# A hybrid encoder block: triangular inverses of two head groups at a time on 128 lanes, and an output projection over all tokens with its inputs finished by heads

## The chip, the core and the metric

The kernel runs on one core of a Trainium2 chip. A core has a matrix engine (TensorE, PE in the profile, with its weight loads listed as PEld), three engines for elementwise work (VectorE or DVE, ScalarE or ACT, GpSimd or POOL), and SyncE (SP), which here only issues transfers. Each engine runs its own instructions in order; semaphores tie them together. Transfers are issued from the queues of SP, POOL and ACT and are carried out by 16 DMA engines. The metric is the device time of one execution in microseconds (us); lower is better.

## The reference

One layer of a block with 512 tokens (S) and 1024 channels (D). After a normalisation, a wide projection `p = h @ w_in` feeds three mixers; their outputs are gated, added and projected, and a squared-ReLU MLP follows:

```python
y_a = b_a * causal_dwconv(c_a * x_a, conv_a_w)
y_b = rg_lru(causal_dwconv(x_b, ...), ...) * gelu(g_b)
yc  = rwkv7_recurrence(r, decay, k, v, kk, a)      # 16 heads of 64
y_c = (layernorm_per_head(yc) * lnx_g + lnx_b + bonus) * g_c
m   = gate_a * y_a + gate_b * y_b + gate_c * y_c
x   = x + m @ w_out
x   = x + square(relu(rms_norm(x) @ mlp_w1)) @ mlp_w2
out = rms_norm(x)
```

The recurrence over tokens is computed in 8 chunks (NC) of 64 tokens (L). Within a chunk it needs, per head, the inverse of a unit triangular 64x64 matrix: 8 chunks times 16 heads are 128 such matrices.

## The kernel before, in words

*Precision.* Every large product is made from three matmuls (`mm3`, L166): the operands are split into a high and a low part, and hi\*hi, hi\*lo, lo\*hi are added. Weights come in tiles of 128x1024: `load_w` (L132) issues the transfer from SP, ScalarE casts the high part `whi` (L146) and VectorE subtracts to get the low part `wlo` (L147, through the helper at L103). There are two raw buffers and three of each part. A projection of 128 output channels (`proj`, L306) is 24 matmuls over 512 tokens into one of three accumulation buffers (`pp`).

*Stages.* The 16 heads are worked on in four groups (NG). For each group, `krv` (L418) projects k, r and v and prepares the scaled operands AR and BK. `amat` (L517) forms the chunk matrices into the tile AXt and writes them to DRAM (`axd`, `bkd`). `inverse(g)` (L546) inverts the group's 32 matrices. Then `chain` (L628) walks through the eight chunks with the state, `norm` (L694) normalises the results in Y after every second chunk, and `fin_m` (L708) turns Y to channels and merges it with the gates. In between, as filler, run `ab(q)` (L744), the first two mixers for each of eight channel tiles q (29 steps each, 232 in all), and `gate(q)` (L726), the projection of the third gate (four steps each). Their results are in the tiles BV and GQ, each in two halves of 256 tokens.

*An inverse.* The 32 matrices of a group lie on lanes: la has one matrix per lane and diagonal block (two blocks of 32x32 per matrix, 64 lanes). Two transposes from AXt fill la (L553). Then 31 substitution steps of two VectorE operations each, a product into dg and a sum into Z, work on all lanes at once (L559 to L568). Three transposes bring the inverses back (L575, L580). The off-diagonal 32x32 block is made on PE by 32 small products pG (L587) and 32 small products pT (L597), each with a copy on ScalarE, and the whole goes to DRAM (`ttd`, L600), from where `load_chunk` reads it per chunk.

*The order of the work.* The program's order is a list by priority, made by hand. `weave(crit, fill, r)` (L823) advances a critical generator by one `yield`, at a raised priority, and then the filler by r steps on average. The filler of an inverse is `fill_group` of the next group (30 steps of `ab`, then `krv` with 9 more among its steps, then 3), at 0.8 steps per step; the last inverse has `ab` steps at 0.85. `N_TT`, `NINV`, `NG_T` are empty steps of the inverse: so many yields lie between its transposes, between the last one and pG, and between pG and pT. `keep_in_program_order` and `pin` fix single instructions in their place. The chain runs with 1.6 filler steps per step over what is left of `ab` and then the gates.

*The output projection* (L900 to L933) is woven by token halves: when the first four chunks are normalised and the gates are done, `fin_m(0, 4)` finishes the first 256 tokens of all heads, and the first three output tiles (W3) are accumulated over them; `fin_m(4, 8)` and the second half follow, then the other five tiles, each as two halves of 256 columns.

Of the kernel before, what the change touches and what calls it, by code (L numbers as in the profile page):

```python
# [18 lines left out]
P = 128  # L19
# [5 lines left out]
N_TT, NINV, NG_T, N_LOAD = 2, 12, 4, 6  # L25


N_KRV = 22
F_INV, F_KRV, F_GAP = 30, 9, 3
W3 = 3  # L30
R0, R1, R2, R3, R4 = 0.85, 0.8, 0.85, 1.6, 1.0
# [66 lines left out]
def block_kernel(ctx, tc, xt, win, par, mulr, sw, wout, w1, w2, fg, cst, eyes, out):  # L98
# [118 lines left out]
    sp = gr_ctx.enter_context(tc.tile_pool(name="sp", bufs=1))  # L217

    HT = S // 2
    HALF = [slice(th * HT, (th + 1) * HT) for th in range(2)]  # L220

    def bv_tile(q, th, dt=F32):
        return sp.tile([P, HT], dt, tag=f"bv{q}{th}", name="bv" if dt == F32 else "ml", align_bytes=AL)
# [194 lines left out]
    def krv(g, G_):  # L418
# [98 lines left out]
    def amat(g, G_):  # L517

        G_.AX = p1.tile([P, 2, NC, 4, L], F32, tag="AXt", name="AXt")
        for c4 in range(2):  # L520
# [10 lines left out]
            yield  # L531
        gp.dma_start(axd[:, 0:64, g, 1].rearrange("c s e t -> s c (e t)"),
# [13 lines left out]
    def inverse(g, G_):  # L546
        AXt = G_.AX
        Z = p1.tile([P, 2, 32, 32], F32, tag="Z", name="Z")
        la, xt = Z[64:128, 0], Z[64:128, 1]
        dg = p1.tile([P, 32, 32], F32, tag="dg", name="dg")  # L550
        tmp = dg[64:128].rearrange("p a b -> p (a b)")
        for b in range(2):
            v.transpose(la[32 * b:32 * b + 32].rearrange("l s t -> l t s"),  # L553
                        AXt[32 * b:32 * b + 32, 0, :, :, 32 * b:32 * b + 32].rearrange("s c e t -> s t (c e)"))
# [576 lines left out]
```

## Time and profile before

| what | value |
|---|---|
| median of three runs | 1103.43 us (1099.84 to 1107.11) |
| the profiled execution's own time | 1100.19 us |
| its span, first to last instruction | 1098.4 us |
| mean granted clock of TensorE | 0.979 |
| moved by DMA | 142.13 MB, mean 129 GB/s |

The profile is one execution. It lists for each engine the busy time and its share of the span, shows the span in 40 equal slices with the busy tenths of each engine, and names groups of instructions by line, engine and operation as `out<-in`, with count, busy time, the mean duration of one in ns, and the idle time before them with what ended it. PEclk is the clock that was granted to TensorE, 9 standing for 0.9 or more. Matmuls are pipelined, so their listed durations overlap; how many run in a stretch of time tells their pace. A line can be a helper's: L103, L106 and L109 are the VectorE helpers, L167 to L169 the three matmuls of `mm3`. A float32 matmul appears as two instructions.

### The profile page before, as it was taken

To read this page: it belongs to the slowest core of one execution; us is meant where nothing else is said; L and a number is where in the kernel's file an instruction comes from. 1 tells how busy PE (TensorE), PEld (TensorE's weight loads), DVE (VectorE), ACT (ScalarE), POOL (GpSimd) and SP (SyncE) were. 2 spreads that over 40 slices of the span, in tenths; PEclk is the share of its full clock that TensorE was granted. 3 is DMA by queue.
4 is the path that set the end of the run, shared out by engine and by line. 5 is a ranking of instruction groups with operands and counts; after the bars stand their busy time and mean duration, and the time that the engine had idled before them with its cause. 6 is when DMAs were issued, how large, how long until landed. Compare 5 with 4: busy or idle time off the path is not lost.

```text
span 1098.4 us, 16103 instructions
## 1 busy us (share of the span) xinstructions
PE 1053.0 (96%) x6396; PEld 863.2 (79%) x6396; DVE 735.3 (67%) x1266; ACT 486.4 (44%) x718; POOL 93.7 (9%) x159
## 2 busy tenths in 40 slices
PE   8999989999999979999699998999999999999996
PEld 5777867787877867788578886998888888888885
DVE  7998987899788987889547777855444443222224
ACT  7755455444573545363445444334444443111114
POOL 0011001110111002200031210101000000000001
PEclk9999989999999989999799999999999999999999
DMA  6336324452446224453288753334332335333232
GB/s 219 120 95 183 100 81 131 130 158 87 138 127 172 82 85 123 123 159 105 70 265 256 252 196 104 116 111 158 96 96 96 96 96 192 96 96 96 95 97 76
DMA packets 43323, 142.13 MB, mean 129 GB/s; under 512 B 5680, under 2 KB 9264, under 8 KB 42224
## 3 DMA queue, kind: packets, MB, share of 16 engines
q1 hardware_dynamic: 29472, 91.02, 25.9%
q0 software_dynamic: 13056, 49.03, 14.8%
q8 instruction: 50, 0.82, 0.3%
q10 hardware_dynamic: 720, 1.05, 0.3%
q14 instruction: 25, 0.20, 0.1%
HBM read 115.91 MB, written 25.17 MB: 128 GB/s over the span
## 4 chain that ended last, share of the span: by engine, by line
PE 47%; DVE 2%; ACT 1%; issue 1%; DMA 0%; DVEq 0%; ACTq 0%
PE acc L167 7%; PE acc L168 7%; PE acc L169 7%; PE p L168 5%; PE p L169 5%; PE p L167 5%; PE pp L167 2%; PE pp L169 2%; PE pp L168 2%; PE py L654 1%; PE pu L644 1%; PE pu L664 1%; PE pS L673 1%; PE pG L587 0%; DVE xr L106 0%
## 5 line engine op out<-in xcount | busy, mean ns | idle before, releaser
L103 DVE TENSOR_TENSOR wlo<-raw,whi 128x1024 fp32r<-128x1024 f32 (+1 forms) x164 | 197.9, 1208 | 228.5 <-ACT whi L146 222.7
L146 ACT CAST whi<-raw 128x1024 fp32r<-128x1024 f32 (+1 forms) x164 | 169.6, 1035 | 274.7 <-PE acc L169 125.0
L167 PE MATMUL pp<-hh,whi 128*128 128x512 f32 x688 | 275.1, 400 | 7.2 <-ACT g L799 4.2
L169 PE MATMUL pp<-hh,wlo 128*128 128x512 f32 x688 | 273.4, 397 | 2.7 <-DVE wlo L103 2.7
L168 PE MATMUL pp<-hl,whi 128*128 128x512 f32 x688 | 273.6, 398 | 0.0
L167 PEld LDWEIGHTS pp<-hh,whi 128*128 128x128 f32 x688 | 131.2, 191 | 37.0 <-ACT g L799 4.8
L169 PEld LDWEIGHTS pp<-hh,wlo 128*128 128x128 f32 x688 | 131.2, 191 | 32.3 <-DVE wlo L103 4.8
L168 PEld LDWEIGHTS pp<-hl,whi 128*128 128x128 f32 x688 | 131.3, 191 | 27.0
L167 PE MATMUL p<-h2h,whi 128*128 128x512 f32 (+1 forms) x264 | 101.4, 384 | 0.0
L168 PE MATMUL p<-h2l,whi 128*128 128x512 f32 (+1 forms) x264 | 101.2, 383 | 0.0
L169 PE MATMUL p<-h2h,wlo 128*128 128x512 f32 (+1 forms) x264 | 101.1, 383 | 0.0
L167 PE MATMUL acc<-whi,ah 128*128 128x512 f32 x256 | 99.6, 389 | 0.0
L168 PE MATMUL acc<-wlo,ah 128*128 128x512 f32 x256 | 99.6, 389 | 0.0
L169 PE MATMUL acc<-whi,al 128*128 128x512 f32 x256 | 99.6, 389 | 0.0
L167 PEld LDWEIGHTS p<-h2h,whi 128*128 128x128 f32 x264 | 49.6, 188 | 9.7
L168 PEld LDWEIGHTS p<-h2l,whi 128*128 128x128 f32 x264 | 49.7, 188 | 9.5
L169 PEld LDWEIGHTS p<-h2h,wlo 128*128 128x128 f32 x264 | 49.6, 188 | 9.6
L169 PEld LDWEIGHTS acc<-whi,al 128*128 128x128 f32 x256 | 48.0, 188 | 10.1
L167 PEld LDWEIGHTS acc<-whi,ah 128*128 128x128 f32 x256 | 48.0, 188 | 10.0
L168 PEld LDWEIGHTS acc<-wlo,ah 128*128 128x128 f32 x256 | 48.0, 188 | 9.9
L103 DVE TENSOR_TENSOR dg<-Z 64x31 f32<-64x31 f32 (+15 forms) x124 | 42.2, 340 | 4.1
L103 DVE TENSOR_TENSOR Z<-Z,dg 64x31 f32<-64x31 f32 (+15 forms) x124 | 42.2, 340 | 4.1
(304 smaller groups left out, 1465.7 us busy)
## 6 DMA issues: line engine op xcount, KB each, us to landing
raw<-in_win SPq DMA_DIRECT2D x88, 512.0 KB, 3.5
raw<-in_w SPq DMA_DIRECT2D x64, 512.0 KB, 3.5
ax<-axd POOLq DMA_DIRECT2D x8, 1024.0 KB, 7.5
axd<-AXt POOLq DMA_DIRECT2D x12, 512.0 KB, 7.1
bkd<-BKT POOLq DMA_DIRECT2D x4, 1024.0 KB, 12.4
raw<-in_wout SPq DMA_DIRECT2D x8, 512.0 KB, 3.6
bk<-bkd POOLq DMA_DIRECT2D x7, 512.0 KB, 8.5
swr<-in_sw SPq DMA_DIRECT2D x16, 128.0 KB, 2.3
```

What stands on the lines that cost most here:

```text
L103: return v.tensor_tensor(out=o, in0=a, in1=b, op=op)
L146: ac.copy(hi[:, sl], raw[:, sl])
L167: pe.matmul(ps, wh, xh, start=start, stop=False)
L168: pe.matmul(ps, wh, xl, start=False, stop=False)
L169: pe.matmul(ps, wl, xh, start=False, stop=stop)
L644: pin(n, lambda: pe.matmul(pu[64 * h:64 * h + 64, x], ax[rows, g, 0, e], sv[rows, g, e], start=True, stop=True))
L654: pin(behind, lambda: pe.matmul(py[64 * h:64 * h + 64, x], w, y, start=first and x == 0, stop=last, skip_group_check=True))
L664: pin(n, lambda: pe.matmul(pu[64 * h:64 * h + 64, x], tc_[:, g, e], u0[:, g, e], start=True, stop=True))
L673: pin(n, lambda: pe.matmul(pS[64 * h:64 * h + 64, x], bk[:, x, 64 * h:64 * h + 64], sv[:, g, e], start=True, stop=True))
```

## The change

Groups are inverted in pairs, on 128 lanes: `inverse(0)` for groups 0 and 1 is woven into the filler of group 2, and `inverse(1)` for groups 2 and 3 stands where the last inverse stood. The list la is no longer made by transposes from AXt. Instead `amat` writes the diagonal blocks of each group to DRAM (`lad`, two transfers of 32 lines by 32 runs of 128 B) and the off-diagonal ones (`odd`, one transfer), and `inverse` loads la from there, with 8 empty steps (`N_LA`) before the first substitution step. One transpose over 128 lanes takes the place of two over 32 for the way back, one over 64 lanes makes d1, and 24 empty steps instead of 12 lie ahead of pG. The small products alternate between the two groups, which lie on different row and column quarters of the array. `ttd` gets another layout; its diagonal blocks are written straight after the transpose, its off-diagonal ones after pT, and its zero blocks once, early.

BV and GQ become tiles of all 512 tokens. `fin_m(g)` finishes the two channel tiles of one group over all tokens. Once the chain's program has ended, it is called after a gate for each group whose gates are done, and for the others after the last gate. The output projection then runs in one piece, eight tiles of 24 matmuls over 512 tokens. The filler shares change with it (`FILL`).

```diff
-N_TT, NINV, NG_T, N_LOAD = 2, 12, 4, 6
-
+N_LA, N_TT, NINV, NG_T, N_LOAD = 8, 1, 24, 4, 6
 
 N_KRV = 22
-F_INV, F_KRV, F_GAP = 30, 9, 3
-W3 = 3
-R0, R1, R2, R3, R4 = 0.85, 0.8, 0.85, 1.6, 1.0
+FILL = {1: (4, 13, 5), 2: (36, 13, 5), 3: (4, 13, 5)}
+
+R0, R1, R2, R3 = 0.85, 0.8, 0.85, 1.6
...
-    ttd = dp.tile([NC, L, NG, 4, L], F32, name="ttd")
+    ttd = dp.tile([L, NG, NC * 4, L], F32, name="ttd")
     vtd = dp.tile([NC, L, NG, 4, L], F32, name="vtd")
+
+    lad = [dp.tile([P, 32, 32], F32, name=f"lad{p_}") for p_ in range(2)]
+    odd = [dp.tile([L, 32, 32], F32, name=f"odd{p_}") for p_ in range(2)]
...
-            BV[2 * g + h] = [bv_tile(2 * g + h, th) for th in range(2)]
-            for th in range(2):
-                tt(BV[2 * g + h][th], pb[:, HALF[th]], vs[h][:, HALF[th]], MUL)
+            BV[2 * g + h] = bv_tile(2 * g + h)
+            tt(BV[2 * g + h], pb, vs[h], MUL)
...
+        gi, pr = g % 2, g // 2
+        ax = G_.AX[:, 0].rearrange("s c e t -> s (c e) t")
+        for b in range(2):
+            r = 64 * b + 32 * gi
+            gp.dma_start(lad[pr][r:r + 32].rearrange("l s t -> s l t"),
+                         ax[32 * b:32 * b + 32, :, 32 * b:32 * b + 32])
+        gp.dma_start(odd[pr][32 * gi:32 * gi + 32], ax[0:32, :, 32:64])
...
-    def inverse(g, G_):
-        AXt = G_.AX
+    def inverse(pr):
+
         Z = p1.tile([P, 2, 32, 32], F32, tag="Z", name="Z")
-        la, xt = Z[64:128, 0], Z[64:128, 1]
+        la, xt = Z[:, 0], Z[:, 1]
         dg = p1.tile([P, 32, 32], F32, tag="dg", name="dg")
-        tmp = dg[64:128].rearrange("p a b -> p (a b)")
-        for b in range(2):
-            v.transpose(la[32 * b:32 * b + 32].rearrange("l s t -> l t s"),
-                        AXt[32 * b:32 * b + 32, 0, :, :, 32 * b:32 * b + 32].rearrange("s c e t -> s t (c e)"))
+        tmp = dg.rearrange("p a b -> p (a b)")
         gp.dma_start(xt.rearrange("l s t -> l (s t)"), eyes)
-
-        yield
-        yield
+        gp.dma_start(la.rearrange("l s t -> l (s t)"), lad[pr].rearrange("l s t -> l (s t)"))
+
+        for _ in range(N_LA):
+            yield
         for s in range(31):
             n, c = 31 - s, s + 1
             tv = tmp[:, 0:n * c].rearrange("l (c t) -> l c t", c=c)
-            mm = tt(tv, la[:, s, s + 1:32].unsqueeze(1).to_broadcast([64, c, n]),
-                    xt[:, 0:c, s:s + 1].to_broadcast([64, c, n]), MUL)
+            mm = tt(tv, la[:, s, s + 1:32].unsqueeze(1).to_broadcast([P, c, n]),
+                    xt[:, 0:c, s:s + 1].to_broadcast([P, c, n]), MUL)
             if s % 3 == 2:
 
                 tc.keep_in_program_order(mm)
             tt(xt[:, 0:c, s + 1:32], xt[:, 0:c, s + 1:32], tv, ADD)
             yield
-        TT = Z[0:64].rearrange("p a b c -> p (a b c)").rearrange("p (l t) -> p l t", t=L)
-        gp.memset(TT[32:64, :, 0:32], 0.0)
-        for b in range(2):
-            for _ in range(N_TT):
-                yield CPI
-            tc.keep_in_program_order(
-                v.transpose(TT[32 * b:32 * b + 32, :, 32 * b:32 * b + 32].rearrange("s l t -> s t l"),
-                            xt[32 * b:32 * b + 32].rearrange("l s t -> l t s")))
+        for _ in range(N_TT):
+            yield CPI
+        TT, od = la, xt[0:64]
+        tc.keep_in_program_order(v.transpose(TT.rearrange("s l t -> s t l"), xt.rearrange("l s t -> l t s")))
+        gp.dma_start(od.rearrange("s l t -> s (l t)"), odd[pr].rearrange("s l t -> s (l t)"))
         for _ in range(N_TT):
             yield CPI
         d1 = gs = dg
-        tc.keep_in_program_order(v.transpose(d1[0:32], TT[0:32, :, 0:32]))
+        tc.keep_in_program_order(v.transpose(d1[0:64], TT[0:64]))
+        for gi in range(2):
+            for b in range(2):
+                r, t = 64 * b + 32 * gi, slice(32 * b, 32 * b + 32)
+                gp.dma_start(ttd[t, 2 * pr + gi, :, t], TT[r:r + 32])
         for _ in range(NINV):
             yield CPI
         for half in range(2):
             pg = pm.tile([P, 16, 32], F32, tag="pm", name="pG")
-            for i in range(16):
-                l = 16 * half + i
-                pin(i, lambda: pe.matmul(pg[32:64, i], AXt[0:32, 0, l // 4, l % 4, 32:64], d1[0:32, l],
-                                             start=True, stop=True))
-            ac.copy(gs[32:64, 16 * half:16 * half + 16], pg[32:64])
+            for n in range(32):
+                i, gi = n // 2, n % 2
+                l, r, o = 16 * half + i, slice(32 * gi, 32 * gi + 32), slice(64 + 32 * gi, 96 + 32 * gi)
+                pin(n, lambda: pe.matmul(pg[o, i], od[r, l], d1[r, l], start=True, stop=True))
+            ac.copy(gs[64:128, 16 * half:16 * half + 16], pg[64:128])
             yield
         for _ in range(NG_T):
             yield 0
         for half in range(2):
             pg = pm.tile([P, 16, 32], F32, tag="pm", name="pT")
-            for i in range(16):
-                l = 16 * half + i
-                pin(i + half, lambda: pe.matmul(pg[0:32, i], gs[32:64, l], TT[32:64, l, 32:64], start=True, stop=True))
-            ac.copy(TT[0:32, 16 * half:16 * half + 16, 32:64], pg[0:32])
+            for n in range(32):
+                i, gi = n // 2, n % 2
+                l, r, o = 16 * half + i, slice(32 * gi, 32 * gi + 32), slice(64 + 32 * gi, 96 + 32 * gi)
+                pin(n + half, lambda: pe.matmul(pg[r, i], gs[o, l], TT[o, l], start=True, stop=True))
+            ac.copy(od[:, 16 * half:16 * half + 16], pg[0:64])
             yield
-        gp.dma_start(ttd[:, :, g].rearrange("c t e x -> t c (e x)"),
-                     TT.rearrange("t (c e) x -> t c (e x)", c=NC))
+        for gi in range(2):
+            gp.dma_start(ttd[0:32, 2 * pr + gi, :, 32:64], od[32 * gi:32 * gi + 32])
...
-        gp.dma_start(flat(tc_), flat(ttd[c]))
+        gp.dma_start(tc_.rearrange("s g e t -> s g (e t)"),
+                     ttd[:, :, 4 * c:4 * c + 4].rearrange("s g e t -> s g (e t)"))
...
-    def fin_m(c_lo, c_hi):
-
-        n, th = c_hi - c_lo, c_lo // 4
-        for g in range(NG):
+    def fin_m(g):
+
+        ys = [C["ph2"].tile([P, S], F32, tag="ym", name="ym", bufs=2) for _ in range(2)]
+        for th in range(2):
             pt = pm.tile([P, 4, P], F32, tag="pm", name="pYt")
-            for i in range(n):
-                pe.transpose(pt[:, i], C["Y"][:, c_lo + i, 2 * g:2 * g + 2].rearrange("p j v -> p (j v)"), ident)
+            for i in range(4):
+                pe.transpose(pt[:, i], C["Y"][:, 4 * th + i, 2 * g:2 * g + 2].rearrange("p j v -> p (j v)"), ident)
             for h in range(2):
-                q = 2 * g + h
-                y = C["ph2"].tile([P, HT], F32, tag="ym", name="ym", bufs=2)
-                tt(y.rearrange("p (c t) -> p c t", t=L), pt[:, 0:n, 64 * h:64 * h + 64],
-                   GQ[q][th].rearrange("p (c t) -> p c t", t=L), MUL)
-                tt(y, y, BV[q][th], ADD)
-                GQ[q][th], BV[q][th] = gq_tile(q, th, F32R), bv_tile(q, th, F32R)
-                ac.copy(GQ[q][th], y)
-                tt(BV[q][th], y, f(GQ[q][th]), SUB)
-            yield
+                tl = slice(HT * th, HT * th + HT)
+                tt(ys[h][:, tl].rearrange("p (c t) -> p c t", t=L), pt[:, :, 64 * h:64 * h + 64],
+                   GQ[2 * g + h][:, tl].rearrange("p (c t) -> p c t", t=L), MUL)
+        for h in range(2):
+            q, y = 2 * g + h, ys[h]
+            tt(y, y, BV[q], ADD)
+            GQ[q], BV[q] = gq_tile(q, F32R), bv_tile(q, F32R)
+            ac.copy(GQ[q], y)
+            tt(BV[q], y, f(GQ[q]), SUB)
+        yield
...
-        GQ[q] = [gq_tile(q, th) for th in range(2)]
-        for th, tl in enumerate(HALF):
-            ac.activation(GQ[q][th], gt[:, tl], AF.Copy, scale=dvp(HLG, q))
-            stt(gt[:, tl], BV[q][th], pv("lb", q), gt[:, tl], ADD, MUL)
-            stt(BV[q][th], gt[:, tl], 0.5, yc[:, tl], MUL, ADD)
+        GQ[q] = gq_tile(q)
+        ac.activation(GQ[q], gt, AF.Copy, scale=dvp(HLG, q))
+        stt(gt, BV[q], pv("lb", q), gt, ADD, MUL)
+        stt(BV[q], gt, 0.5, yc, MUL, ADD)
...
-        for _ in range(F_INV):
+        lead, among, gap = FILL[g]
+        for _ in range(lead):
             next(fl, None)
             yield
         acc = 0.0
         for _ in krv(g, GS[g]):
             yield
-            acc += F_KRV / N_KRV
+            acc += among / N_KRV
             while acc >= 1.0:
                 acc -= 1.0
                 next(fl, None)
                 yield
-        for _ in range(F_GAP):
+        for _ in range(gap):
             next(fl, None)
             yield
 
     weave(krv(0, GS[0]), fl, R0)
+
+    for g in range(NG):
+        gp.dma_start(ttd[32:64, g, :, 0:32], zer[0:32, 0:32].unsqueeze(1).to_broadcast([32, NC * 4, 32]))
     for g in range(NG):
         if g:
             fgr = fill_group(g)
-            weave(inverse(g - 1, GS[g - 1]), fgr, R1, CPV)
+            if g == 2:
+                weave(inverse(0), fgr, R1, CPV)
             drain(fgr)
         weave(amat(g, GS[g]), fl, 1.0)
-    weave(inverse(NG - 1, GS[NG - 1]), fl, R2, CPV)
+    weave(inverse(1), fl, R2, CPV)
...
+        done = 0
         for q in range(KT):
             yield from gate(q)
+            while C["c"] == NC and done < (q + 1) // 2:
+                yield from fin_m(done)
+                done += 1
...
-        while C["c"] < 4:
-            yield
-        yield from fin_m(0, 4)
-        M["half"] = True
-        yield from w_out_first()
-
-    def w_out_mm(mo, w, acc, th):
-        for q in range(KT):
-            mm3(acc[:, HALF[th]], *wslice(w, q), GQ[q][th], BV[q][th], start=q == 0, stop=q == KT - 1)
+        while done < NG:
+            if C["c"] == NC:
+                yield from fin_m(done)
+                done += 1
+            else:
+                yield
...
-    def w_out_first():
-
-        M["w"], M["acc"] = [], []
-        for mo in range(W3):
+    def w_out():
+        for mo in range(KT):
             w = load_w(wout[mo])
             acc = pp.tile([P, S], F32, tag="pp", name="acc")
-            w_out_mm(mo, w, acc, 0)
-            M["w"].append(w)
-            M["acc"].append(acc)
-            yield
-
-    def w_out_rest():
-        for mo in range(W3):
-            w_out_mm(mo, M["w"][mo], M["acc"][mo], 1)
-            w_out_end(mo, M["acc"][mo])
-            yield
-        for mo in range(W3, KT):
-            w = load_w(wout[mo])
-            acc = pp.tile([P, S], F32, tag="pp", name="acc")
-            for th in range(2):
-                w_out_mm(mo, w, acc, th)
+            for q in range(KT):
+                mm3(acc, *wslice(w, q), GQ[q], BV[q], start=q == 0, stop=q == KT - 1)
             w_out_end(mo, acc)
-            yield
...
-    def end():
-        while "half" not in M:
-            yield
-        yield from fin_m(4, 8)
-
     fc = fill_chain()
     weave(chain(), fc, R3)
-    weave(end(), fc, R4)
     drain(fc)
-    drain(w_out_rest())
+    w_out()
...
-    z["eyes"] = np.tile(np.eye(32, dtype=np.float32).reshape(1, 1024), (64, 1))
+    z["eyes"] = np.tile(np.eye(32, dtype=np.float32).reshape(1, 1024), (P, 1))
```

More of the change, by code (lines that the diff above doesn't have):

```diff
@@ L219, in block_kernel, with bv_tile @@
     HT = S // 2
-    HALF = [slice(th * HT, (th + 1) * HT) for th in range(2)]
-    def bv_tile(q, th, dt=F32):
-        return sp.tile([P, HT], dt, tag=f"bv{q}{th}", name="bv" if dt == F32 else "ml", align_bytes=AL)
+    def bv_tile(q, dt=F32):
+        return sp.tile([P, S], dt, tag=f"bv{q}", name="bv" if dt == F32 else "ml", align_bytes=AL)
     BV = [None] * KT
@@ L871, in block_kernel, with gq_tile @@
     GQ = [None] * KT
-    def gq_tile(q, th, dt=F32):
-        return C["ph2"].tile([P, HT], dt, tag=f"gq{q}{th}", name="gq" if dt == F32 else "mh", align_bytes=AL)
+    def gq_tile(q, dt=F32):
+        return C["ph2"].tile([P, S], dt, tag=f"gq{q}", name="gq" if dt == F32 else "mh", align_bytes=AL)
     C["Y"] = C["ph2"].tile([P, NC, 8, L], F32, name="Y")
```

## The prediction

> **What bounds the kernel now.** I read the page first: engine shares, the slices and the chain that ended last.
>
> ```profile
> span 1098.4 us, 16103 instructions
> PE 1053.0 (96%) x6396; PEld 863.2 (79%) x6396; DVE 735.3 (67%) x1266; ACT 486.4 (44%) x718; POOL 93.7 (9%) x159
> ...
> PE   8999989999999979999699998999999999999996
> ...
> PEclk9999989999999989999799999999999999999999
> ```
>
> TensorE (PE) is busy 96% of the span, so a saving must shorten what PE executes or the time in which it stands or runs at a lowered clock. The dents of the PE row (the sixth, fifteenth, twentieth and twenty-fifth slice) mostly coincide with dents of PEclk, the clock granted to it. A busy share does not show lost throughput, so next I counted PE's instructions in stretches around the dents, with two quiet stretches for scale (a row gives the stretch, its length, PE's busy time and instructions, the mean granted clock, the DMA share and GB/s).
>
> ```profile
> 140.00:180.00 40.00, 35.26 (x239) 0.87 0.26 80
> 260.00:280.00 20.00, 17.90 (x78) 1.00 0.31 96
> 390.00:420.00 30.00, 24.33 (x169) 0.83 0.23 82
> 520.00:550.00 30.00, 20.78 (x185) 0.77 0.25 79
> 680.00:690.00 10.00, 5.54 (x30) 0.84 0.35 113
> 705.00:735.00 30.00, 30.00 (x252) 1.00 0.32 109
> 760.00:920.00 160.00, 160.00 (x707) 1.00 0.32 99
> ```
>
> In 760 to 920 us nothing but 512-column matmuls runs: 160/707 = 0.2263 us each. In 705 to 735 us only the output projection's 256-column ones run: 30/252 = 0.1190 each. The small ones of the inverse come from these rows:
>
> ```profile
> L587 PE MATMUL pG<-dg,AXt 32*32 32x32 f32 x256 | 11.9, 211 | 12.2 <-DVE dg L580 9.2 <-ACT a L442 3.0
> L597 PE MATMUL pT<-Z,dg 32*32 32x32 f32 x256 | 9.5, 192 | 0.0
> 390.00:420.00 30.00, 1.19 (x32) 0.83 0.23 82
> 535.86 3.59 PE pG L587 x64
> ...
> 543.16 0.42 PE pp L168
> 543.58 0.24 PE pp L169
> ...
> 545.86 1.12 PE pT L597 x32
> 577.28 1.08 PE py L654 x32
> ```
>
> The first two are groups of the whole run, 64 of each per inverse; the third is the pT line alone in that stretch; the rest are pieces of the chain of waits (start, length). A small matmul takes 1.12/32 = 0.035 us. Lost per stretch is its length less what its instructions need:
>
> - 140 to 180: 128 small and 111 wide, 4.5 + 25.1 = 29.6, lost 10.4
> - 260 to 280: 78 wide, 17.7, lost 2.3
> - 390 to 420: 96 small and 73 wide, 3.4 + 16.5 = 19.9, lost 10.1
> - 520 to 550: 128 small and 57 wide, 4.5 + 12.9 = 17.4, lost 12.6
>
> These are the tails of the four inverses: 35.4 us. The waits name the causes.
>
> ```profile
> PE pG L587 <- DVE dg L580: 9.2, 1, 9.2
> PE pp L167 <- ACT g L799: 4.2, 1, 4.2
> PE pG L587 <- ACT a L442: 3.0, 2, 2.5
> PE pYt L714 <- DVE gc L106: 2.8, 1, 2.8
> ...
> PE acc L167 <- ACT mh L722: 1.5, 1, 1.5
> ```
>
> The worst is the last inverse: pG is next in PE's order, its operand dg is the last of three transposes on DVE, and PE stands 9.2 us. Then it runs at half speed: from 535.86 to 543.58 everything takes about twice as long (a wide matmul 0.42 instead of 0.24), which costs another 3.9. The 4.2 has the same root: ScalarE's copy that frees PE's buffer waits, through a gate's activation, on a DVE product that lies behind the transposes. The entry of the output projection waits 2.8 + 1.5, and at clock 0.84 in 680 to 690 us loses 1.6 more: 5.9.
>
> **The change part by part.** First the DVE work of an inverse.
>
> ```profile
> L103 DVE TENSOR_TENSOR dg<-Z 64x31 f32<-64x31 f32 (+15 forms) x124 | 42.2, 340 | 4.1
> L103 DVE TENSOR_TENSOR Z<-Z,dg 64x31 f32<-64x31 f32 (+15 forms) x124 | 42.2, 340 | 4.1
> L553 DVE STREAM_TRANSPOSE Z<-AXt 32x1024 f32<-32x1024 f32 x8 | 16.8, 2099 | 0.2
> L575 DVE STREAM_TRANSPOSE Z<-Z 32x1024 f32<-32x1024 f32 x8 | 16.5, 2069 | 0.2
> L580 DVE STREAM_TRANSPOSE dg<-Z 32x1024 f32<-32x1024 f32 x4 | 4.9, 1229 | 0.1
> L103 DVE TENSOR_TENSOR dg<-Z 64x255 f32<-64x255 f32 x8 | 3.4, 422 | 0.3
> L103 DVE TENSOR_TENSOR swbl<-swr,swbh 128x256 fp32r<-128x256 f32 x8 | 3.4, 424 | 1.3 <-ACT swbh L406 1.2
> ```
>
> *Joint lanes.* A 64-lane operation of 255 elements takes 422 ns, a 128-lane one of 256 takes 424: lanes are free. Two joint inverses need 42 us of steps instead of 84. The transposes from AXt vanish (16.8), those at the end become one of about 2.07 per pair instead of four (16.5 to 4.1), dg's two of 1.23 instead of four. DVE loses 42 + 16.8 + 12.4 + 2.5 = 74 us. DVE is at 67% of the span and not its bound, so the 74 us themselves count for nothing; what counts is the tail, where DVE holds 2.1 + 1.2 = 3.3 us instead of 5.4 and twice instead of four times. Also 24 steps instead of 12 lie between dg and pG: at 0.85 filler steps of six wide matmuls (1.36 us) each that is 27.7 us of PE work instead of 13.9, and 13.8 more cover the 9.2. Bounds of what a joint tail still loses: 0 (all hidden) and 12.6 (as now at worst). The second inverse loses 2.3 with the same work; I take 3.5 each, nearer to it, as the cover doubles: 7.0 instead of 35.4: **-28.4**.
>
> *pG and pT.* 128 pairs become 128 pairs with groups alternating over row and column quarters: 512 instructions before and after, 0. The Trainium skill's TensorEngine Tiling (Array Packing), Overview, says that small tiles of the array can run side by side, up to four times faster at 32. The trace speaks against it at this issue rate: py's matmuls alternate both halves of the array and take 1.08/32 = 0.034 each, no less than pT on one tile. By the rule halved, the sum would be 9.0 lower.
>
> *The list's detour.* New on POOL: per group three writes of 1024 pieces of 128 B (lad twice, odd), four writes of zeros, per pair the loads of la and od, six ttd writes instead of two, against two fewer eyes: 26 more issues.
>
> ```profile
> L485 POOL DMA_DIRECT2D rtd<-AR x8 | 7.3, 915 | 122.2 <-DVE rqq L109 52.1 <-DVE rqq L103 39.2 <-DVE spt L392 15.6
> bkd<-BKT POOLq DMA_DIRECT2D x4, 1024.0 KB, 12.4
> rtd<-AR POOLq DMA_DIRECT2D x8, 256.0 KB, 3.2
> Z<-in_eyes POOLq DMA_DIRECT2D x4, 256.0 KB, 3.4
> ```
>
> rtd has 1024 pieces too and takes 0.915 us of POOL: 24 us more on an engine at 9%, hidden. What is not hidden by construction is la, which amat's masks, two writes and a load precede. Low: 2 x 0.9 + 3.2 + 3.4 = 8.4 us. High, queued like bkd both times: 1.8 + 12.4 + 12.4 = 26.6. The cover is 8 x 0.8 = 6.4 steps, 8.7 us. So DVE's first multiply stands between 0 and 18 us, and behind it in DVE's order lie the weight splits (wlo) and every evacuation that PE's buffers wait for. The load is nearest to bkd in its place, as it follows bkd and three axd writes in POOL's order; I take about 10 us of DVE standing, of which PE, which has three weight buffers and so one or two projections of 24 wide matmuls (5.4 us) in hand, feels 3 us a pair: **+6** (0 to 36, and half speed on top). od has the 27.7 us above as cover against at most 12.4; tc's load reads shorter runs off the path. By the Trainium skill's DMA: Bandwidth & Descriptors, Anatomy of one DMA, a transfer takes about 2.0 us plus its bytes at 436 GB/s; with its estimate la would arrive inside the cover, and the 6 would be 0. The bkd row, 12.4 us for 1 MB behind three others, differs from it.
>
> *Output projection.* 384 matmuls of 0.1190 (45.7) become 192 of 0.2263 (43.4): **-2.3**. Bounds 0 and -2.3.
>
> *Heads finished between gates.* The chain's program has 34 steps with 1.6 filler steps each, 54. Before, 24 steps of the branches and 32 of the gates were left for it; now, with 195 of 232 branch steps spent earlier instead of 208, 37 + 32 = 69. So the chain ends some four gates early, and three of four groups are finished under the gates' projections. Only heads 6 and 7 follow the last gate, and six of eight accumulation steps can run before them. Entry 5.9 to 1.5 (bounds 0 and 5.9): **-4.4**. The merged DVE and ACT operations save a little on engines off the path: 0.
>
> Sum: -28.4 + 6 - 2.3 - 4.4 = -29.1. The profiled execution took 1100.2, so 1071; its time is 0.3% under the median 1103.4, and the three runs span 7 us, so I leave it at that.
>
> **Rivals.** (a) The joint tails stay as bad as three of the four now, (10.4 + 10.1 + 12.6)/3 = 11 each: -13.4 + 6 - 2.3 - 4.4 = -14.1, 1086. For it: DVE is as full in the second group; against: less transposing, longer filler. (b) Nothing of tails and entry is left and la is in time: -35.4 - 2.3 - 5.9, 1057. For it: the quiet stretches between tails lose nothing. (c) la comes late both times: DVE stands 18 us, its splits are not ahead, PE stands as long and then loses 3.9 at half speed: 2 x 21.9 = 43.8 - 28.4 - 2.3 - 4.4 = +8.7, 1109, slower. It decides from 17.6 us a pair. For it the bkd row; against, splits that run ahead. (d) The steps don't mesh and the chain still ends after the gates, so no head is finished earlier and the entry stays: 1075. (e) Quarter tiles overlap after all: 1062; the py row speaks against.
>
> **How the numbers follow.** Forecast 1071: 0.52; (a) 0.20; (b) 0.10; (c) 0.08; (d) 0.06; (e) 0.04. A measurement tells about 1% from no change, so faster is below 1092. Of the forecast, (a) and (c) I put 0.02, 0.03 and 0.05 inside 1%, of (c) 0.03 beyond, and small scatter besides: faster 0.85, same 0.11, slower 0.04. The range, 1053 to 1096, leaves out (c) and the far side of (b).
>
> **What would show it.** Right: DVE busy near 660; two pG stretches instead of four, with PE waiting under 4 us for dg; no PE dent near 680 us; acc on 128x512, x192; PE waits of a few us for wlo shortly after the second and fourth amat, while DVE waits for the la load. Wrong: DVE standing 15 us for Z; pG waits of 9 us again; pYt all after the last gate; small matmuls clearly under 0.035.

## The result, and the profile after

The changed kernel takes 1047.39 us (median of four runs, 1045.94 to 1048.35), the kernel before 1105.27 us in the same series (four runs): a ratio of 0.9478, 95% interval 0.9432 to 0.9524. The profiled execution took 1047.99 us, 52.2 less than the one of before. The forecast was 1071, 29.1 less, and its range began at 1053: the sign is right, the size is not.

The page of the changed kernel, its engines, PE's slices and the clock:

```profile
span 1045.8 us, 15536 instructions
PE 1023.8 (98%) x6204; PEld 833.4 (80%) x6204; DVE 647.1 (62%) x1086; ACT 479.7 (46%) x694; POOL 111.0 (11%) x181
...
PE   8999999999999999999999999999999999999996
...
PEclk8999999999999999999999999999999999999998
```

All four dents are gone, the three that belong to tails of inverses and the one at the entry of the output projection, and with them the three of the clock. The waits of PE, longest first:

```profile
PE pst L271 <- DVE sq L102: 2.8, 2, 2.1
PE tp L938 <- ACT sj L944: 2.3, 1, 2.3
PE pB L548 <- DVE AXt L102: 2.3, 3, 1.1
PE wu L255 <- POOL one L252: 1.5, 1, 1.5
PE pn L452 <- ACT a L443: 1.2, 1, 1.2
```

No wait of pG and none of pYt is left. The stretches of the two joint inverses (columns as in the prediction's: stretch, length, busy time and instructions of PE, PEld, DVE, ACT and POOL, clock, DMA share, GB/s):

```profile
200.00:250.00 50.00, 50.00 (x222) 41.35 (x222) 43.80 (x93) 24.98 (x34) 0.66 (x2) 1.00 0.34 112
250.00:270.00 20.00, 20.00 (x323) 16.24 (x322) 18.05 (x35) 13.22 (x20) 6.61 (x10) 1.00 0.61 165
420.00:460.00 40.00, 40.00 (x178) 33.06 (x177) 38.23 (x85) 22.15 (x32) 0.56 (x1) 1.00 0.29 96
460.00:480.00 20.00, 20.00 (x207) 16.62 (x206) 12.32 (x16) 8.60 (x14) 4.26 (x6) 1.00 0.49 150
```

PE is busy through both tails. The small matmuls, by the timeline of PE (start, length, count):

```profile
257.90 2.21 PE L594 MATMUL pG<-dg,Z 32*32 32x32 f32 x128
...
265.48 1.20 PE L604 MATMUL pT<-Z,dg 32*32 32x32 f32 x64
...
472.75 2.21 PE L594 MATMUL pG<-dg,Z 32*32 32x32 f32 x128
```

They take 2.21/128 = 0.017 and 1.20/64 = 0.019 us each, half of before's 0.035. Where the 52.2 us came from, by counting as the prediction did (length of a stretch less what its instructions need):

| term | before | after | gained |
|---|---|---|---|
| the tails of the inverses | 35.4 | about 0 | 35.4 |
| the 512 small matmuls | 512 x 0.035 = 17.9 | 2 x 2.21 + 4 x 1.20 = 9.2 | 8.7 |
| entry of the output projection | 5.9 | 0.3 | 5.6 |
| its columns | 45.7 | 43.4 | 2.3 |

That makes 52.0. The table's 0.035 for a small matmul holds for pT as it is listed; e1 below has the same 512 at 16.3 us. Other stretches shift by up to 4 us in both directions (the start loses more, the stretches around amat less) and cancel.

### The profile page after: what moved, and what is told of

Read it like the earlier page. It is cut to its first block, busy times and chain, and to the rows that moved or that the text cites. A ratio compares the mean times of both kernels' runs of the same rounds, so it can differ in the third digit from the quotient of the medians.

```text
span 1045.8 us, 15536 instructions
## 1 busy us (share of the span) xinstructions
PE 1023.8 (98%) x6204; PEld 833.4 (80%) x6204; DVE 647.1 (62%) x1086; ACT 479.7 (46%) x694; POOL 111.0 (11%) x181
## 4 chain that ended last, share of the span: by engine, by line
PE 86%; DVE 10%; issue 2%; ACT 1%; DMA 1%; SPq 0%; DVEq 0%; ACTq 0%
PE pp L166 13%; PE pp L167 13%; PE pp L168 13%; PE acc L166 7%; PE acc L167 7%; PE acc L168 7%; PE p L167 5%; PE p L166 5%; PE p L168 5%; DVE wlo L102 2%; PE py L662 1%; PE pu L652 1%; PE pu L672 1%; DVE rk L105 1%; PE pB L548 1%
## 5 line engine op out<-in xcount | busy, mean ns | idle before, releaser
L166 PE MATMUL pp<-hh,whi 128*128 128x512 f32 x688 | 271.0, 394 | 0.4 <-DVE rs L105 0.4
L167 PE MATMUL pp<-hl,whi 128*128 128x512 f32 x688 | 270.1, 393 | 0.0
L168 PE MATMUL pp<-hh,wlo 128*128 128x512 f32 x688 | 269.1, 391 | 0.2 <-DVE wlo L102 0.2
L166 PEld LDWEIGHTS pp<-hh,whi 128*128 128x128 f32 x688 | 129.1, 188 | 28.6 <-DVE rs L105 0.9
L167 PEld LDWEIGHTS pp<-hl,whi 128*128 128x128 f32 x688 | 129.2, 188 | 26.4
L992 ACT CAST ah<-r 128x512 fp32r<-128x512 f32 x32 | 19.9, 622 | 43.4 <-DVE r L102 43.4
L102 DVE TENSOR_TENSOR al<-r,ah 128x512 fp32r<-128x512 f32 x32 | 22.2, 692 | 21.5 <-ACT ah L992 21.4
```

Of the source, the lines that this page charges most:

```text
L102: return v.tensor_tensor(out=o, in0=a, in1=b, op=op)
L166: pe.matmul(ps, wh, xh, start=start, stop=False)
L167: pe.matmul(ps, wh, xl, start=False, stop=False)
L168: pe.matmul(ps, wl, xh, start=False, stop=stop)
L992: ac.copy(ahi, r)
```

## The experiments

Each was timed in three rounds against the kernel before (e9 in five); a ratio is to that kernel. A difference between a run and the change is one between medians of different series, in which the kernel before itself came out at 1103.0 to 1105.6 us. The ratio intervals of e2 and e7 lie clear of the change's (0.9432 to 0.9524); those of e1, e3, e4, e5, e9 and e11 overlap it, so their differences of 3 to 7 us are likely, and what shows them is the waits and paces in the traces. The question behind most of them was what carried the tails away. The theory formed on seeing the result: inside the inverses' stretches VectorE (DVE) is as good as the bound, whatever its share of the span is; what it is behind by is collected in its queue and paid in the tail, where PE needs dg. The rival is the prediction's view: the tail is a wait of its own, made by three transposes and a short cover.

### e12: half the steps of the kernel before

```diff
         for s in range(31):
+            if s % 2:
+                yield
+                continue
             n, c = 31 - s, s + 1
```

> The kernel before, with every odd substitution step of its four inverses left out (its place in the order stays, as an empty step): 15 of 31 steps, about 41 us of VectorE work, as much as the joint lanes take away. The inverses that come out are not inverses. Number of tails (four), transposes (five per inverse), cover (12 empty steps), PE's work and the detour-free list stay as before. Theory (inside the inverses' stretches VectorE is the bound; what it is behind by is paid in the tails): its 10 us less per inverse are paid back there: 25 to 35 of the 35 us of the tails go, no PE wait for dg above 3 us, 1068 to 1082. Rival (the prediction's view: what counts is the tail itself, its transposes, their number and the cover; VectorE's work on the steps counts for nothing): the tails keep 20 us or more: 1088 to 1105.

Measured: 1076.2 us (1074.59 to 1079.99), ratio 0.9744 (0.9705 to 0.9784), 29 less than before. The engines on its page, its longest waits of PE, and the stretches of the tails:

```profile
PE 1047.5 (97%) x6396; PEld 860.7 (80%) x6396; DVE 692.4 (64%) x1146; ACT 486.1 (45%) x718; POOL 93.4 (9%) x159
```

```profile
PE pYt L717 <- DVE gc L106: 2.9, 1, 2.9
...
PE pG L590 <- DVE dg L583: 1.6, 1, 1.6
```

```profile
140.00:170.00 30.00, 30.00 (x214) 24.14 (x213) 19.99 (x34) 19.51 (x28) 0.90 (x1) 0.94 0.32 97
260.00:280.00 20.00, 20.00 (x136) 16.19 (x135) 10.39 (x12) 10.56 (x16) 0.00 (x0) 0.93 0.41 129
380.00:410.00 30.00, 30.00 (x237) 24.32 (x237) 23.94 (x40) 15.62 (x22) 2.90 (x5) 1.00 0.41 122
510.00:540.00 30.00, 27.32 (x246) 22.46 (x247) 12.12 (x15) 11.25 (x15) 6.14 (x11) 0.94 0.52 172
```

Four tails, all the transposes and the short cover are still there; 43 us of DVE's work have gone (735.3 to 692.4) and with them 29 us by the medians, 23 by the two profiled executions (spans 1098.4 and 1075.1). The wait of 9.2 us for dg is 1.6. Counted as in the prediction, with the small matmuls that fall into these stretches (107, 64, 128 and 128, and 32 of the chain in the last), they lose 2.0, 1.5, 0.9 and 4.9 us, together 9 instead of 35.4: 26 us back, at the lower end of the theory's 25 to 35, of which by the spans some 3 are lost again elsewhere. The time lies in the theory's range, too. So DVE's work on the steps does count, against the rival, and it is most of the tails. One thing went with the steps: five of the ten products per inverse that `keep_in_program_order` holds in their place.

### e7: the change with its lanes taken apart

```diff
-            mm = tt(tv, la[:, s, s + 1:32].unsqueeze(1).to_broadcast([P, c, n]),
-                    xt[:, 0:c, s:s + 1].to_broadcast([P, c, n]), MUL)
...
-            tt(xt[:, 0:c, s + 1:32], xt[:, 0:c, s + 1:32], tv, ADD)
+            for k, hs in enumerate((slice(0, 64), slice(64, 128))):
+                mm = tt(tv[hs], la[hs, s, s + 1:32].unsqueeze(1).to_broadcast([64, c, n]),
+                        xt[hs, 0:c, s:s + 1].to_broadcast([64, c, n]), MUL)
...
+                tt(xt[hs, 0:c, s + 1:32], xt[hs, 0:c, s + 1:32], tv[hs], ADD)
```

> The changed kernel with each substitution step done in two operations of 64 lanes instead of one of 128, so that the two joint inverses cost 84 us of steps on DVE again; joint transposes, cover, detour and output part stay. Theory (the joint lanes count, since DVE is at 97% between 220 and 260 us): the steps end 15 to 20 us later, more than the 7 us that dg had in hand, and PE waits about 10 us in each tail and loses half speed behind it, 1065 to 1080. Rival (the cover and the shorter transposes carry the tails, the 42 us of steps lie beside PE's work): 1047 to 1051.

Measured: 1098.37 us (1095.92 to 1100.73), ratio 0.9933 (0.991 to 0.9956): 51 us more than the change, for DVE work of 692.5 instead of 647.1 us. More than either side expected. Its longest wait of PE and three stretches:

```profile
PE pp L166 <- ACT u L816: 26.9, 2, 14.3
```

```profile
250.00:270.00 20.00, 7.40 (x27) 5.63 (x25) 19.00 (x48) 8.18 (x13) 0.00 (x0) 0.66 0.22 67
270.00:290.00 20.00, 18.52 (x258) 14.96 (x256) 19.65 (x36) 10.21 (x14) 5.21 (x7) 1.00 0.44 121
490.00:510.00 20.00, 5.66 (x20) 4.24 (x19) 19.18 (x44) 8.71 (x12) 0.89 (x2) 0.66 0.26 83
```

In 250 to 270 and 490 to 510 us DVE is busy 95% of the time and PE about a third of it: PE stands up to 14.3 us at a time for a ScalarE copy of the filler, and ScalarE, ahead of that copy, stands for products of DVE (7.1, 2.7 and 1.6 us in a row before 265 us). No wait for dg is left among PE's waits, where the theory had put them: the arrears come out ahead of the tail, at the first thing that PE needs from DVE. With two joint inverses, double cover, two tails and everything else as in the change, almost the whole gain is gone. So the gain hangs on 128 lanes taking DVE no longer than 64; joining two inverses into one tail is worth little without that. The 51 us are not the price of this work in the kernel before, though: there it was spread over four inverses' steps, here it stands in two, beside about half the filler.

### e2 and e6: the cover of empty steps

```diff
-N_LA, N_TT, NINV, NG_T, N_LOAD = 8, 1, 24, 4, 6
+N_LA, N_TT, NINV, NG_T, N_LOAD = 8, 1, 12, 4, 6
```

> The changed kernel with 12 empty steps instead of 24 between the last transpose and pG, as before the change. In the changed kernel dg is ready at 251.3 and 465.5 us and pG runs at 257.9 and 472.8; 12 steps fewer move pG about 13 us ahead in PE's order. Theory (the long cover carries the tails): PE waits 6 to 7 us for dg in each tail and then runs some us at half speed, 1062 to 1068. Rival (the freer DVE alone carries them, dg simply comes earlier): waits under 2 us, 1047 to 1050.

Measured for e2, the change with the short cover: 1059.3 us (1057.39 to 1059.92), ratio 0.9578 (0.9563 to 0.9592), 12 more than the change and between the sides, nearer to the theory. Its waits show pG late again, behind other work of DVE:

```profile
PE pG L594 <- DVE g L105: 4.3, 1, 4.3
...
PE pG L594 <- DVE u L105: 3.2, 1, 3.2
```

The other way round, e6 is the kernel before with NINV 24 instead of 12:

> The kernel before with 24 empty steps instead of 12 between an inverse's last transpose and pG, nothing else. Theory (the tails were lost because DVE is full with four inverses on half the lanes, and cover moves the wait elsewhere): of the 35 us in the tails at most a third goes, 1090 to 1103. Rival (the distance between dg and pG is what the change brought): the 9.2 us wait and half speed after it go, and the other tails too, some 25 us, about 1080.

Measured: 1090.87 us, ratio 0.9868 (0.9827 to 0.9909), as the theory had it: 12 less than before by the medians of this series, 8 by the two profiled executions (spans 1098.4 and 1090.3). The loss of the last tail falls from 13 to 2.5 us, the first and third keep about 9 and 10. Up to the start of the chain (563 us here, 564 before) PE runs 59 more wide matmuls, 13 us of work, so about 14 us of loss have gone there; by the spans some 6 come back behind it, where these filler steps are missing (PE waits 3.9 us for the normalised Y). So the cover is worth about 12 us in the change and 8 to 12 in the kernel before. Neither the cover nor the lighter steps (23 to 29 by e12) gives all that the change gets from its inverses. No run puts the two together on the kernel before; nor does one test by themselves the 31 us of transposes that DVE loses with the change (38.2 in the prediction's rows, 6.9 after).

### e10: the kernel before with more filler per step

```diff
-R0, R1, R2, R3, R4 = 0.85, 0.8, 0.85, 1.6, 1.0
+R0, R1, R2, R3, R4 = 0.85, 1.15, 1.2, 1.6, 1.0
```

> The kernel before with the filler of its inverses raised from 0.8 to 1.15 steps per step (0.85 to 1.2 for the last), nothing else: each VectorE step of an inverse stands beside 1.4 times the matmuls. Theory (VectorE is the bound inside the inverses' stretches, and what it is behind by falls on the tails): more PE work per step takes away the lag, the tails' 35 us fall to 10 to 20, no pG wait above 5 us: 1078 to 1094. Rival (the tail is a wait of its own, three transposes and a copy, as the prediction has it): three tails keep 8 us or more of their loss, and the cover of 12 empty steps grows from 13.9 to 19.6 us of PE work, which only the last one feels: 1094 to 1104.

Measured: 1102.89 us (1100.5 to 1104.56, ten runs), ratio 0.9982 (0.9958 to 1.0006): no difference. The time is the rival's, the theory's missed. Waits of PE and three stretches:

```profile
PE pYt L714 <- DVE Y L103: 9.4, 1, 9.4
PE pn L451 <- ACT a L442: 5.9, 3, 2.7
```

```profile
395.00:430.00 35.00, 27.44 (x121) 20.97 (x120) 33.25 (x69) 19.88 (x29) 3.17 (x6) 1.00 0.35 103
...
680.00:690.00 10.00, 4.84 (x128) 4.32 (x128) 3.95 (x5) 1.75 (x3) 0.00 (x0) 0.79 0.01 2
690.00:700.00 10.00, 3.22 (x14) 2.85 (x15) 7.27 (x23) 1.80 (x3) 0.00 (x0) 0.50 0.00 0
```

The wait of pG for dg is gone, as the theory had it. But this filler brings DVE work of its own, so DVE stays at 33.25 of 35 us ahead of the third tail, and other instructions wait: up to the start of the chain (580 us here, 564 before) PE runs 120 more wide matmuls, 27 us of work, in 16 us more, so no more than 11 to 12 us of loss have gone. And the steps used up there are missing under the chain: 640 to 710 us loses some 21 instead of 8 us, with a wait of 9.4 us for the normalised Y and the clock at 0.50 around its end. The loss moved rather than went. Between theory and rival this run decides nothing, since it changed DVE's load along with PE's.

### e1: pG and pT with the tiles one after the other

The same line in both loops, of pG and of pT:

```diff
-                i, gi = n // 2, n % 2
+                i, gi = n % 16, n // 16
```

> The changed kernel with the small products pG and pT in another order: all 16 of one group, then all 16 of the other, so that neighbours use the same quarter of the array; count, shapes and everything else stay. Theory (neighbouring products on different quarters overlap): the pace of pG goes from 2.21 us for 128 back to about 0.035 each, 4.4 us, and 512 small ones cost 512 x (0.035 - 0.017) = 9 us more, so about 1056 us. Rival (the new tile operands or the clock made the pace, the order doesn't matter): within 2 us of the changed kernel's 1047.

Measured: 1052.41 us (1051.04 to 1053.51), ratio 0.953 (0.9498 to 0.9561), 5.0 more than the change. The same instructions on the same tiles, in another order; the timeline of PE:

```profile
256.07 3.93 PE L594 MATMUL pG<-dg,Z 32*32 32x32 f32 x128
...
265.37 2.11 PE L604 MATMUL pT<-Z,dg 32*32 32x32 f32 x64
```

Together 2 x 3.93 + 4 x 2.11 = 16.3 us instead of 9.2. Here matmuls of 32x32 overlap when neighbours in PE's order lie on different quarters of the array, and not when they lie on the same one. The quarters differ in rows and in columns at once; which of the two it takes is not tested. The order of the change is what makes the overlap: 7 us on PE, where the theory had 9, and 5 between the medians.

### e3: no empty steps ahead of the first multiply

```diff
-N_LA, N_TT, NINV, NG_T, N_LOAD = 8, 1, 24, 4, 6
+N_LA, N_TT, NINV, NG_T, N_LOAD = 0, 1, 24, 4, 6
```

> The changed kernel with no empty step (N_LA 0 instead of 8) before the first substitution step. The load of la takes 14 us to land, and in the changed kernel DVE reaches its first multiply some 20 us after the load was issued. Theory (the order on DVE is laid out so that the multiply comes after the modelled landing, whatever N_LA is; and splits run ahead of PE): the multiply waits under 5 us a pair, time within 3 us of 1047. Rival (as the prediction had it: DVE stands for the rest of the load, and PE with it): DVE stands about 10 us a pair and PE loses 6 or more in all, 1053 or above.

Measured: 1054.03 us, ratio 0.9545 (0.9514 to 0.9575), 6.6 more than the change. The two rows that decide the question of la, in the change: its load on POOL's queue, and DVE's first multiply.

```profile
189.48 0.57 POOL L560 DMA_DIRECT2D Z<-lad  x1
```

```profile
208.53 0.74 DVE L105 SCALAR_TENSOR_TENSOR u<-u,part,u 128x511 f32<-128x511 f32 x1
209.19 0.18 DVE L102 TENSOR_TENSOR dg<-Z 128x31 f32<-128x31 f32 x1
```

The load takes 14.4 us and is there by 204; DVE comes to the multiply at 209.19 straight from other work and waits for nothing. Without the empty steps it comes at 206.9, still not waiting. The 6.6 us are lost at the other end, where pG waits:

```profile
PE pG L594 <- DVE u L105: 3.1, 1, 3.1
...
PE pG L594 <- DVE wlo L102: 2.8, 1, 2.8
```

Without them pG comes earlier in PE's order, and the steps hardly start earlier on DVE; so eight empty steps ahead of the substitution are cover for the tail too. Neither side had this: the theory's mechanism (DVE doesn't stand for la) holds, its bound on the time doesn't.

### e8, e4, e5 and e11: the output projection

e8 is the output part of the change alone, on the kernel before, with its inverses as they were; e11 is the inverse part alone, with halves of 256 tokens behind it. e4 and e5 take one thing out of the whole change:

In e4:

```diff
-            while C["c"] == NC and done < (q + 1) // 2:
-                yield from fin_m(done)
-                done += 1
```

In e5:

```diff
-            for q in range(KT):
-                mm3(acc, *wslice(w, q), GQ[q], BV[q], start=q == 0, stop=q == KT - 1)
+            for th in range(2):
+                tl = slice(th * HT, th * HT + HT)
+                for q in range(KT):
+                    mm3(acc[:, tl], *wslice(w, q), GQ[q][:, tl], BV[q][:, tl], start=q == 0, stop=q == KT - 1)
```

> The kernel before with the output part of the change alone: BV and GQ as tiles of all tokens, fin_m by groups between the gates where the chain has ended, the projection in one piece of 512 columns; inverses, ttd and the filler shares as before. Theory (the parts add up: 2.3 from the columns, while the chain still ends with the gates, so that all heads are finished after it and the entry stays as long or longer): 1098 to 1108, no clear difference from before. Rival (the output part carries its 8 us by itself): 1095 to 1097, below before by 0.7%.

> The changed kernel with no head finished between the gates: all four fin_m come after the last gate, everything else stays. Theory (the place between the gates is what takes the entry away): the first group needs its transposes, products and splits after the last gate while PE has nothing, and each further group about 4.4 us of DVE for 4.1 us of PE over three output tiles, 5 to 8 us more, 1052 to 1056. Rival (it is enough that the chain ended before the gates): within 2 us of 1047.

> The changed kernel with each output tile accumulated in two halves of 256 columns again, 384 matmuls of 0.119 instead of 192 of 0.226. Theory: 2.3 us more, about 1050. Rival (the heads that come last feed the halves in another order and PE waits): 1052 or more; or nothing at all, if weight loads were not what cost: 1047.

> The inverse part of the change alone on the kernel before: joint lanes, quarter tiles, the detour through DRAM; gates, fin_m and the output projection stay in halves of 256 tokens. Theory: nearly all of the 58 us comes from here; missing are the 2.3 us of the columns and 3 to 6 us of the entry, as the two runs with half columns and with heads last showed each by itself: 1051 to 1057, PE busy above 96%, pYt waits of 2 to 5 us. Rival: the two parts need each other (the output part alone gave nothing because the chain ended with the gates; here it ends earlier without use), so the parts don't add up: above 1060, or below 1049.

| kernel | us | ratio to before (95%) |
|---|---|---|
| e8, output part alone | 1104.17 | 0.9996 (0.9971 to 1.0022) |
| e4, change with all heads finished last | 1050.73 | 0.9503 (0.9482 to 0.9523) |
| e5, change with half columns | 1052.44 | 0.9516 (0.9502 to 0.953) |
| e11, inverse part alone | 1053.99 | 0.9533 (0.9498 to 0.9567) |

Alone the output part gives nothing, as its theory had it; behind the joint inverses it gives 6.6 us by the medians (1053.99 less 1047.39). In e8 the chain ends with the gates, and its longest wait of PE for an inverse is the one of before:

```profile
PE pG L584 <- DVE dg L577: 9.9, 1, 9.9
```

In the change the transposes pYt stand between the gates, at 609.51 to 643.75 us. With all heads finished last, 3.3 us come back by the medians and 4.9 by the profiled executions (1052.87 and 1047.99), with two waits for them:

```profile
PE pYt L722 <- DVE gc L105: 1.6, 1, 1.6
...
PE pYt L722 <- DVE ym L102: 0.9, 1, 0.9
```

That is between the sides (5 to 8, and under 2). The half columns cost 5.0 by the medians, 2.5 by the profiled executions. Their length is 2.3 of it, and there is a wait of 2.4 for the first finished head, as its rival had it:

```profile
PE acc L166 <- ACT mh L731: 2.4, 1, 2.4
```

Between that run's theory (about 1050) and its rival (1052 or more) this does not decide. e11 came inside its theory's bounds, with a wait of pYt of 1.6 us, under the 2 to 5 that it named.

### e9: a version of the change

```diff
-                st = M["xrp"].tile([P, S], F32, tag="st", name="st", bufs=2)
+                st = M["xrp"].tile([P, S], F32, tag="st", name="st", bufs=4)
...
-            if fi == 0:
-                for th in range(2):
-                    mlp1(t, w, slice(th * HT, (th + 1) * HT))
-            else:
-                mlp1(t, w, slice(0, S))
+            mlp1(t, w, slice(0, S))
```

> The changed kernel with two small edits behind the output projection: the tile st of the change to tokens has four buffers instead of two, and the first tile of the MLP is made over 512 columns at once instead of two halves. Theory: PE's wait of 2.3 us for sj goes, since the transposes' squares no longer hold the buffers, and 24 matmuls of 0.226 take the place of 48 of 0.119, 0.3 us: 1044.5 to 1046 beside 1047.4 in the same runs, ratio to before 0.945 to 0.9465. Rival: the squares on ScalarE are the pace there, so the wait moves to the first product of the MLP, which needs all 512 tokens at once: 1047 to 1049.

Measured: 1043.48 us (1042.43 to 1046.8, five runs), ratio 0.9436 (0.9406 to 0.9465). The wait for sj no longer appears among PE's waits, and the span is 1040.7. The interval overlaps that of the change (0.9432 to 0.9524), so 2 to 4 us are likely and not shown; the median lies 1 us under the theory's range, and the rival's is missed.

## Why the prediction was right in sign and wrong in size

The profiled gain is 52.2 us, 23.1 more than the forecast's 29.1. Step by step:

- *The tails, -28.4.* Gained 35.4: the 3.5 us that each joint tail was to keep are not there. That the doubled cover helps was right (12 us by e2, 8 to 12 by e6). The step that failed is "DVE is at 67% of the span and not its bound, so the 74 us themselves count for nothing". Rows of the kernel before show what the share of the span hides. They are the stretches that lead into the waits of the first and the last tail, and between them the one ahead of the second tail, which loses little:

```profile
130.00:150.00 20.00, 17.09 (x76) 13.78 (x74) 18.84 (x36) 8.09 (x12) 0.00 (x0) 1.00 0.25 86
240.00:260.00 20.00, 20.00 (x90) 16.57 (x89) 19.03 (x35) 14.45 (x20) 0.00 (x0) 1.00 0.26 86
510.00:530.00 20.00, 16.64 (x74) 13.44 (x72) 19.01 (x33) 10.22 (x15) 0.00 (x0) 0.99 0.28 83
```

  DVE is busy 94% to 95% in all three, and PE 85%, 100% and 83%. DVE runs its queue in order: the steps, the filler's weight splits and gates, then the transposes, and what it is behind by comes out at whatever PE needs from it next. In the last tail that is dg (9.2 us). In the first it is ScalarE's copy g (4.2 us), which stands 3.7 us for a DVE product behind the transposes; in the third it is DVE's ks (2.6 us). That the work is what counts is shown by the runs: e12 takes 43 us of it away for 23 to 29, and e7 puts 45 back into the change for 51. A full DVE alone loses nothing, as the middle row shows; the changed kernel, too, has it at 38.23 of 40 us in 420 to 460, and PE at 40.00, and with half the cover behind it pays 12 us (e2). Work and cover have to be read together; the prediction had the cover alone. Rival (a), 11 us a tail, was wrong for the same reason. (b), nothing left of the tails and of the entry with la in time, was the right picture of these terms, and so was (e) of the small matmuls; the prediction weighed them one at a time, and (b) with the 9.0 of (e) makes 1048, against the measured 1047.
- *The small matmuls, 0.* Gained 8.7, of which e1 shows 7.1 on PE and 5.0 between the medians. The step that failed is "The trace speaks against it at this issue rate". The py row speaks for it, read closely: py's matmuls move 64 columns and pT's 32, so equal mean times are no sign of equal pace. In the trace of the kernel before, py's starts come in pairs, 6 to 7 ns apart and then 51 to 52, while pT's come evenly, every 31 to 32 ns. The change's pG starts in pairs as py does (6 to 7, then 25). So py overlapped already. The Trainium skill's TensorEngine Tiling (Array Packing), Overview, has small tiles side by side; the trace agrees, with 1.8 times on two quarters (16.3 against 9.2 us, e1).
- *The list's detour, +6.* Measured 0. The load was as long as the neighbour row said, near bkd's:

```profile
Z<-lad POOLq DMA_DIRECT2D x2, 512.0 KB, 14.4
lad<-AXt POOLq DMA_DIRECT2D x8, 128.0 KB, 3.1
...
bkd<-BKT POOLq DMA_DIRECT2D x4, 1024.0 KB, 13.7
```

  The step that failed is the cover, "8 x 0.8 = 6.4 steps, 8.7 us": from the load's issue at 189.48 to the multiply at 209.19 are 19.7 us, because DVE had other work standing in its order ahead of it, some of it waiting in turn for a weight's high part (4.86 us up to 204.06), and it comes straight from that work even with no empty step at all (e3). By the Trainium skill's DMA: Bandwidth & Descriptors, Anatomy of one DMA, 512 KB would take an estimated 3.2 us; the trace differs, with 14.4. The 0 that the prediction drew from that page came true for another reason than the page's.
- *Columns, -2.3.* In agreement with the counts, 45.7 and 43.4; e5, which takes them back, costs 5.0 by the medians and 2.5 by the profiled executions.
- *Heads finished between the gates, -4.4.* Measured 5.6, its mechanism as described. It hangs on the filler shares, as the prediction's count of 69 steps against 54 has it: with the inverses and shares of before (e8) the chain ends with the gates, and the output part is worth nothing.
- *What would show it.* Two pG stretches, acc over 512 columns and no dent at the entry came as written; DVE's 647.1 is 13 under "near 660". The waits for wlo behind la did not come, and the small matmuls "clearly under 0.035", named as a sign of error, did.

Of the 23.1 us, 8.7 are the overlap, 7.0 the tails, 6 la, 1.2 the entry. How the 35.4 us of the tails divide between cover and DVE's work stays open: lighter steps alone give 26 in the tails (e12), cover alone 8 to 12 in the time (e6), and the two may overlap.

## What to carry to other kernels

Read the bound by stretch and by engine, above all ahead of a dent: an engine at 67% of the span can be at 95% where it matters, and its queue hands the arrears to whoever needs a result of it next. A busy share alone does not tell whether that costs time; taking work away from the stretch, as e12 does, tells it. Work taken off DVE in such stretches was worth more than half of its own time (23 to 29 us for 43), which is what an operation on more lanes for the same time buys; and empty steps between a result and its use were worth 8 to 12 us for 12 steps, as long as the filler that they use up is not needed later. For how long a late load is covered, take the distance from its issue to its use in the trace, not the steps that the program names.

## What the runs showed of the hardware that was not expected

- Matmuls of 32x32 on alternating quarters of the array take 0.017 to 0.019 us each, the same ones in turn on one quarter 0.031 to 0.033 (e1); only the order differs.
- The granted clock was low also where PE stood for a filler: 0.66 in stretches in which PE was busy 7.40 and 5.66 of 20 us (e7). In e10 it was 0.50 from 690 to 700 us, six of them in the wait of 9.4 us and four behind it.
